# Decay factors of a state-space scan on ScalarE, a mask kept in PSUM, and a logits product widened from 64 to 128 rows

## The chip, the core and the metric

The kernel runs on one core of one Trainium2 chip. TensorE, VectorE, ScalarE, GpSimd and SyncE each work through their own queue in order; in this kernel every DMA is issued from SyncE's queue. The metric is the device time of one launch in microseconds.

## What is computed

One layer of a hybrid encoder is evaluated for 512 prompt tokens and 32 sample tokens that share the weights: an input projection, a banded attention with 16 heads of 64 columns (A), a Mamba-2 state-space scan with 32 heads in 4 groups (B), gates and an output projection, a convolutional feed-forward part and a last gated product. Two pieces matter here. The scan, per chunk and group, is

```python
acs = jnp.cumsum(ac, axis=1)
seg = acs[:, :, None] - acs[:, None, :]
decay = jnp.where(tri, jnp.exp(jnp.where(tri, seg, 0.0)), 0.0)
cb = jnp.einsum('bign,bjgn->bijg', cc, bc)
y = jnp.einsum('bijg,bijgr,bjgrp->bigrp', cb, decay, dx)
y = y + jnp.einsum('bign,bgrpn->bigrp', cc, hc) * jnp.exp(acs)[..., None]
```

and the attention logits are

```python
logits = jnp.einsum('bihd,bjhd->bhij', q, k) * (HEAD_DIM_A ** -0.5)
probs = jax.nn.softmax(logits + bias[None], axis=-1)
```

## The kernel before

All large products run on TensorE with activations as features by tokens (128 x 544). A fp32 weight block of 128 x 1024 (a unit) is split into a rounded high part `wh` (ScalarE, line 250) and a rest `wl` (line 254, on VectorE, or on GpSimd for the odd ones of the first 40 units), and each product is three passes: high by high, high by low, low by high (`mm3`, line 273). One chunk of dense work is six such matmuls of 272 columns; a step of eight chunks fills a PSUM tile `dps` (two buffers), which an epilogue then reads. TensorE's order is written out by hand (`Ordered` pins every matmul behind the one before). The order on the other engines, and which buffer of a pool a tile gets, is the framework's choice: it lists instructions by the time at which it thinks they can start.

The scan runs inside the dense work (lines 1128 to 1142). For each of 20 pairs of group and token block, `ssd_a` (line 611) is emitted, then 7 dense chunks, then `ssd_b` (line 663) of the pair before, then 6 dense chunks. `ssd_a` makes C-by-B in a PSUM tile `cbt`, multiplies it by the triangle into `cbm` in SBUF (line 625), splits the transposed B (lines 627 and 628), and then, for each half of 4 heads: loads the cumulated decay rows `ab` by DMA, broadcast to all partitions (line 647); forms `min(ab - acs, 0)` for 4 heads on VectorE (line 651); one exp on ScalarE (line 652); one product with `cbm` on VectorE (line 653); for all but the first block also exp of `ab` and its product with C on GpSimd (lines 657 and 658). `ssd_b` uses these tiles in its matmuls `yps` and `st`. The half tiles (`dx`, `wj`, `wjh`, `wjl`, `ab`, `m`) share 14 buffers; the PSUM tiles `cbt`, `xst`, `yps`, `st` and all small ones later share 4 buffers (`sps`, line 172).

The attention follows, again between dense chunks (lines 1144 to 1169). For a pair of heads m, `stack` (line 806) builds `qs` (the rounded query in one half of the 128 rows, its rest in the other half) and `ks` (the rounded key in both halves, the second copied there by DMA), and `kl` (the key's rest, in the head's own 64 rows, line 820). One tile `kl` serves both heads. `att_a` (line 823) makes the logits of a block of 128 queries and n = 256, 384 or 512 keys with two matmuls per head: `qs` by `ks` on 128 rows (line 848) and `qs` by `kl` on the head's own 64 rows (line 849), both into the same PSUM tile. The softmax, the transposes (`att_b`) and the product with V (`att_c`) come in later slots, with dense chunks between them (`FILL`).

`bias_vector` (line 551) builds a vector of relative-position biases once, in a constant tile `er`, and writes it to DRAM (`evec`).

Of the kernel before, what the change touches and what calls it, by code (L numbers as in the profile page):

```python
# [9 lines left out]
F32 = mybir.dt.float32  # L10
F32R = mybir.dt.float32r
AF = mybir.ActivationFunctionType
ALU = mybir.AluOpType
MUL, ADD, SUB, MAX, MIN = ALU.mult, ALU.add, ALU.subtract, ALU.max, ALU.min
# [16 lines left out]
EROW = 640  # L31
# [85 lines left out]
def trunk(ctx: ExitStack, tc: tile.TileContext, a):  # L117
    nc = tc.nc
    V, S, G = nc.vector, nc.scalar, nc.gpsimd
# [15 lines left out]
    PE = Ordered()  # L135
# [4 lines left out]
    const = ctx.enter_context(tc.tile_pool(name="const", bufs=1))  # L140
# [6 lines left out]
    pools = {"sp": sp_stack.enter_context(tc.tile_pool(name="sp", bufs=1))}  # L147
# [6 lines left out]
    def slot(dt=F32, name="t", src=None):  # L154
        src = free_slots if src is None else src
        pool, i = src.popleft()
        t = pool.tile([128, T], dt, tag=f"t{i}", name=name, bufs=1)
        held[id(t)] = (t, pool, i, src)
        return t

    def done(*ts):
        for t in ts:
            _, pool, i, src = held.pop(id(t))
            src.append((pool, i))
# [10 lines left out]
    def spt(shape, tag, bufs):  # L175
        return pools["sp"].tile(shape, F32, tag=tag, name=tag, bufs=bufs)
# [372 lines left out]
        dense.defer(4, bias_vector)  # L549

    def bias_vector():
        er = const.tile([16, EROW], F32, name="er")
        nc.sync.dma_start(er[:, 383:EROW], a["rb"])
        V.tensor_scalar(er[:, 383:EROW], er[:, 383:EROW], -1.0, None, op0=MUL)
        V.tensor_copy(er[:, 0:383], er[:, 383:384].to_broadcast([16, 383]))
        nc.sync.dma_start(evec, er)
        for h in range(16):
            dense.defer(16 + 16 * h, lambda h=h: bias_rows(h))

# [51 lines left out]
    def ssd_a(g, c):  # L611
        q0 = 128 * c
        Q = 128 if c < 4 else SMP
        tk = slice(q0, q0 + Q)
        b, cc = bc["B", g], bc["C", g]
        if c == 4:
            hst = spt([128, 512], "h", 4)
            nc.sync.dma_start(hst, a["hT"][:, 512 * g : 512 * g + 512])
            state[g, "s"] = hst
        inter = c != 0  # L620
        sm = sps("cbt")
        PE.matmul(sm[:Q, 0:Q], lhsT=b[:, tk], rhs=cc[:, tk], start=True, stop=True)
        PE.transpose(sm[:Q, 128:256], b[:, tk], ident)
        cbm = spt([128, 128], "cbm", 2)
        V.tensor_tensor(cbm[:Q, :Q], sm[:Q, 0:Q], tri[:Q, :Q], op=MUL)
        bth, btl = (pools["sp"].tile([128, 128], F32R, tag=n, name=n, bufs=2) for n in ("bth", "btl"))
        S.copy(bth[:Q], sm[:Q, 128:256])
        V.tensor_tensor(btl[:Q], sm[:Q, 128:256], bth[:Q].bitcast(F32), op=SUB)
        xp = sps("xst")
        for i in range(4):  # L630
            PE.transpose(xp[:Q, 128 * i : 128 * i + 128], xs[4 * g + i][:, tk], ident)
        dx = half_tile("dx")
        wj = half_tile("wj")
        xv = xp.rearrange("p (h f) -> p h f", f=64)
        for dst, i in ((dx, 0), (wj, 2)):
            V.tensor_tensor(dst.rearrange("p a (b f) -> p (a b) f", f=64)[:Q], xv[:Q],  # L636
                            tm[:Q, i, c, 8 * g : 8 * g + 8].unsqueeze(2).to_broadcast([Q, 8, 64]), op=MUL)
        dxf = dx.rearrange("p a b -> p (a b)")
        wjh, wjl = half_tile("wjh", F32R), half_tile("wjl", F32R)
        S.copy(wjh[:Q], wj[:Q])  # L640
        G.tensor_tensor(wjl[:Q], wj[:Q], wjh[:Q].bitcast(F32), op=SUB)
        sts = [(l[:Q], r.rearrange("p a b -> p (a b)")[:Q]) for l, r in ((bth, wjh), (bth, wjl), (btl, wjh))]
        ms, cps = [], []
        for hh in range(2):
            ab = half_tile("ab")
            src = asc[c, 8 * g + 4 * hh : 8 * g + 4 * hh + 4, 0:Q]
            nc.sync.dma_start(ab[:, :, :Q], src.unsqueeze(0).to_broadcast([128, 4, Q]))
            m = half_tile("m")
            for i in range(4):
                hd = 8 * g + 4 * hh + i  # L650
                V.tensor_scalar(m[:Q, i, :Q], ab[:Q, i, :Q], tm[:Q, 1, c, hd : hd + 1], 0.0, op0=SUB, op1=MIN)  # L651
            S.activation(m[:Q, :, :Q], m[:Q, :, :Q], AF.Exp)  # L652
            V.tensor_tensor(m[:Q, :, :Q], m[:Q, :, :Q],  # L653
                            cbm[:Q, :Q].unsqueeze(1).to_broadcast([Q, 4, Q]), op=MUL)
            ms.append(m)
            if inter:
                S.activation(ab[:, :, :Q], ab[:, :, :Q], AF.Exp)  # L657
                G.tensor_tensor(ab[:, :, :Q], ab[:, :, :Q],  # L658
                                cc[:, tk].unsqueeze(1).to_broadcast([128, 4, Q]), op=MUL)
                cps.append(ab)  # L660
        return dxf, sts, ms, cps
# [122 lines left out]
    bias = {}  # L784

    def att_load(m):
        if m not in att:
            att[m] = slot(name="at", src=at_slots)
        if m % 2 == 0:
            bs = qk["bs", m] = apt([128, NKS], "bs", 1)  # L790
            for p in range(2):
                ck = qk["ck", m + p] = apt([128, PAST], "ck", 2)
                nc.sync.dma_start(ck, a["ck"][m + p])
                cv = qk["cv", m + p] = apt([128, 2, 128], "cv", 2)
                nc.sync.dma_start(cv, a["cv"][m + p])
            for j in range(4):
                nc.sync.dma_start(bs[32 * j : 32 * j + 32], toeplitz(2 * m + j, SMP, 255, NKS))
        for hi in range(2):
            b = apt([128, 512], "bias", 4)
            nc.sync.dma_start(b, toeplitz(2 * m + hi, 128, 127, 512))  # L800
            G.memset(b[0:64, 448:512], -NEG)
            bias[m, hi] = b

    stk = {}

    def stack(m, hi):
        q, k = qk["q", m], qk["k", m]

        def st(n, tag):
            return pools["ap"].tile([128, n], F32R, tag=tag, name=tag, bufs=1)  # L810

        kl = st(512, "kl") if hi == 0 else stk[0][2]
        a0, b0 = 64 * hi, 64 - 64 * hi
        own, oth = slice(a0, a0 + 64), slice(b0, b0 + 64)
        qs, ks = st(384, f"qs{hi}"), st(512, f"ks{hi}")
        S.copy(ks[own], k[own, 0:512])
        nc.sync.dma_start(ks[oth].bitcast(F32), ks[own].bitcast(F32))
        S.copy(qs[own], q[own, 128:512])
        V.tensor_tensor(qs[oth], q[own, 128:512], qs[own].bitcast(F32), op=SUB)
        G.tensor_tensor(kl[own], k[own, 0:512], ks[own].bitcast(F32), op=SUB)  # L820
        stk[hi] = qs, ks, kl

    def att_a(m, i):
        q, k = qk["q", m], qk["k", m]
        if i < 0:
            L = sps("Ls")
            for s in (0, 1):
                for j in range(4):
                    mm, own = m + j // 2, slice(64 * (j % 2), 64 * (j % 2) + 64)
                    r = qk["k", mm][own, SEQ:T] if s else qk["ck", mm][own, :]  # L830
                    PE.matmul(L[32 * j : 32 * j + 32, PAST if s else 0 : NKS if s else PAST],
                              lhsT=qk["q", mm][own, SEQ:T], rhs=r, start=True, stop=True)
            P = apt([128, NKS], "Ps", 1)
            softmax(P, L[:, :NKS], qk["bs", m], 128)
            return [P]
        n = 128 * (i + 1)
        Ps = []
        Ls = []
        for hi in range(2):
            p0 = 64 * hi  # L840
            L = sps("L")
            own = slice(p0, p0 + 64)
            if i == 0:
                PE.matmul(L[:, :n], lhsT=q[own, 0:n], rhs=k[own, 0:n], start=True, stop=True)
            else:
                qs, ks, kl = stk[hi]
                sl = slice(n - 256, n - 128)
                PE.matmul(L[:, :n], lhsT=qs[:, sl], rhs=ks[:, 0:n], start=True, stop=False)
                PE.matmul(L[:, :n], lhsT=qs[own, sl], rhs=kl[own, 0:n], start=False, stop=True)
            Ls.append(L)  # L850
        for hi in range(2):
            P = apt([128, 512], "P", 4)
            softmax(P[:, :n], Ls[hi][:, :n], bias[m, hi][:, 512 - n : 512], 128)
            Ps.append(P)
        return Ps
# [289 lines left out]
            (1, 0): (4, 3), (1, 1): (3, 4), (1, 2): (4, 3), (1, 3): (1, 3)}  # L1145
    todo = [(m, i) for m in range(NPAIR) for i in range(-1 + m % 2, 4)]
    prev = None
    att_load(0)
    stack(0, 0)
    dense.run(11)  # L1150
# [113 lines left out]
```

## Time and profile before

| what | value |
|---|---|
| median of three runs | 1412.58 us (1412.04 to 1417.83) |
| profiled execution, its own time | 1413.28 us |
| its span, first to last instruction | 1411.2 us |
| busy: TensorE, VectorE, ScalarE, GpSimd | 98%, 65%, 43%, 25% of the span |
| mean granted clock of TensorE | 0.991 of 2.4 GHz |

The busy share of TensorE is modelled from pipelined matmuls, so it is read by stages, and beside it the distance from the start of one matmul to the start of the next. Three stages are told apart here: the scan (74 to 381 us), the attention (381 to 640 us) and the dense rest.

### The profile page before, as it was taken

To read this page: it belongs to the slowest core of one execution; us is meant where nothing else is said; L and a number is where in the kernel's file an instruction comes from. 1 tells how busy PE (TensorE), PEld (TensorE's weight loads), DVE (VectorE), ACT (ScalarE), POOL (GpSimd) and SP (SyncE) were. 2 spreads that over 40 slices of the span, in tenths; PEclk is the share of its full clock that TensorE was granted. 3 is DMA by queue.
4 is the path that set the end of the run, shared out by engine and by line. 5 is a ranking of instruction groups with operands and counts; after the bars stand their busy time and mean duration, and the time that the engine had idled before them with its cause. 6 is when DMAs were issued, how large, how long until landed. Compare 5 with 4: busy or idle time off the path is not lost.

```text
span 1411.2 us, 26759 instructions
## 1 busy us (share of the span) xinstructions
PE 1376.0 (98%) x11065; PEld 1324.1 (94%) x11065; DVE 916.0 (65%) x1654; ACT 613.4 (43%) x1016; POOL 352.1 (25%) x464
## 2 busy tenths in 40 slices
PE   7998898989999999999999999999999999999998
PEld 7997897989988888889999999999999999999998
DVE  7999999996865555564355334577777537753545
ACT  5444343455566666654244223344444214432342
POOL 5466475464422112210000000023333103310000
PEclk9999999999999999999999999999999999999999
DMA  5723232323443323311222332222222232222221
GB/s 175 241 90 109 87 120 64 116 92 110 132 138 114 103 88 99 103 64 61 90 91 90 122 122 90 91 78 79 85 88 91 90 106 90 91 93 90 90 90 65
DMA packets 41929, 142.16 MB, mean 101 GB/s; under 512 B 9264, under 2 KB 13248, under 8 KB 29520
## 3 DMA queue, kind: packets, MB, share of 16 engines
q1 hardware_dynamic: 41808, 140.46, 29.6%
q8 instruction: 87, 1.43, 0.4%
q14 instruction: 34, 0.28, 0.1%
HBM read 129.27 MB, written 14.31 MB: 102 GB/s over the span
## 4 chain that ended last, share of the span: by engine, by line
PE 81%; DVE 13%; DMA 2%; ACT 2%; issue 1%; POOL 1%; SPq 0%; POOLq 0%; ACTq 0%
PE dps L130 72%; DVE m L651 3%; PE L L130 3%; DVE cv L597 2%; PE O L130 2%; DMA ab<-asc 2%; PE Tp L133 1%; DVE m L653 1%; DVE wl L254 1%; PE yps L130 1%; DVE xs L684 1%; DVE dx L636 1%; DVE wj L636 0%; PE qn L130 0%; DVE h L693 0%
## 5 line engine op out<-in xcount | busy, mean ns | idle before, releaser
L130 PE MATMUL dps<-hi,wh 128*128 128x272 f32 x2960 | 627.9, 294 | 14.9 <-DVE ext L572 14.6
L130 PE MATMUL dps<-lo,wh 128*128 128x272 f32 x2960 | 616.2, 290 | 5.3 <-DVE lo L375 5.3
L130 PE MATMUL dps<-hi,wl 128*128 128x272 f32 x2960 | 615.4, 290 | 2.3 <-DVE wl L254 1.9
L130 PEld LDWEIGHTS dps<-hi,wh 128*128 128x128 f32 x2960 | 467.4, 190 | 26.2 <-issue 18.5
L130 PEld LDWEIGHTS dps<-lo,wh 128*128 128x128 f32 x2960 | 469.0, 190 | 6.1 <-DVE lo L375 6.1
L130 PEld LDWEIGHTS dps<-hi,wl 128*128 128x128 f32 x2960 | 467.8, 189 | 3.1 <-DVE wl L254 2.5
L250 ACT CAST wh<-wr 128x1024 fp32r<-128x1024 f32 x192 | 201.2, 1048 | 379.3 <-PE dps L130 339.4
L254 DVE TENSOR_TENSOR wl<-wr,wh 128x1024 fp32r<-128x1024 f32 x173 | 213.3, 1233 | 48.2 <-ACT wh L250 43.3
L597 DVE SCALAR_TENSOR_TENSOR cv<-ext,hv,cv 128x547 f32<-128x547 f32 x72 | 76.9, 1068 | 2.7 <-ACT cv L594 2.1
L1021 DVE SCALAR_TENSOR_TENSOR ucv<-uext,vec,ucv 128x546 f32<-128x546 f32 x96 | 75.4, 785 | 4.2 <-ACT ucv L1018 2.4
L1014 POOL COPY cfo<-uext 128x2 f32<-128x2 f32 x48 | 10.4, 217 | 262.4 <-DVE uext L571 262.4
L1011 POOL MEMSET uext<- 128x2 f32 x48 | 4.6, 95 | 281.2 <-issue 281.2
L1053 DVE TENSOR_TENSOR x<-x,dps 128x544 f32<-128x544 f32 x24 | 17.3, 722 | 78.2 <-PE dps L130 78.0
L651 DVE TENSOR_SCALAR m<-ab,tm 128x128 f32<-128x128 f32 (+1 forms) x160 | 63.2, 452 | 5.3 <-DMA ab<-asc 5.3
L777 DVE CUSTOM_DVE_ANT_0 P<-L,bias 128x128 f32<-128x128 f32 (+3 forms) x64 | 30.9, 483 | 53.7 <-PE L L130 53.2
L569 DVE TENSOR_TENSOR uext<-dps,rstd 128x272 f32<-128x272 f32 x48 | 21.2, 442 | 63.1 <-PE dps L130 58.5
L254 POOL TENSOR_TENSOR wl<-wr,wh 128x1024 fp32r<-128x1024 f32 x19 | 50.8, 2672 | 44.8 <-ACT wh L250 36.8
L1015 POOL COPY cfo<-uext 128x2 f32<-128x2 f32 x48 | 55.5, 1157 | 0.0
L658 POOL TENSOR_TENSOR ab<-ab,bc 128x512 f32<-128x512 f32 (+1 forms) x32 | 42.5, 1332 | 40.1 <-ACT ab L657 37.8
L652 ACT ACTIVATE m<-m 128x512 f32<-128x512 f32 (+1 forms) x40 | 22.7, 567 | 65.8 <-DVE m L651 65.6
L733 POOL TENSOR_TENSOR ql<-qs,qh 128x544 fp32r<-128x544 f32 x16 | 22.0, 1376 | 103.6 <-ACT qh L732 91.6
L779 ACT ACTIVATE P<-P,sm 128x128 f32<-128x128 f32 (+3 forms) x64 | 36.0, 562 | 23.2 <-DVE sm L777 22.9
(246 smaller groups left out, 1626.4 us busy)
## 6 DMA issues: line engine op xcount, KB each, us to landing
wr<-in_w SPq DMA_DIRECT2D x96, 1024.0 KB, 4.9
ab<-asc SPq DMA_DIRECT2D x32, 256.0 KB, 5.5
bsc<-evec SPq DMA_DIRECT2D x16, 320.0 KB, 7.5
bias<-bsc SPq DMA_DIRECT2D x16, 256.0 KB, 3.5
xin<-in_xT SPq DMA_DIRECT2D x8, 272.0 KB, 5.4
out_o_v<-v SPq DMA_DIRECT2D x8, 272.0 KB, 2.1
out_o_k<-qk SPq DMA_DIRECT2D x8, 272.0 KB, 2.1
x<-in_xT SPq DMA_DIRECT2D x8, 272.0 KB, 4.6
```

Source lines behind the costliest of these rows:

```text
L130: return self._pin(nc.tensor.matmul(*args, **kw))
L250: cp = S.copy(hi, r)
L254: eng.tensor_tensor(lo, r, hi.bitcast(F32), op=SUB)
L597: V.scalar_tensor_tensor(y[:, :n], ext[:, j : j + n], hv[:, 24 * j + ti : 24 * j + ti + 1], y[:, :n], op0=MUL, op1=ADD)
L651: V.tensor_scalar(m[:Q, i, :Q], ab[:Q, i, :Q], tm[:Q, 1, c, hd : hd + 1], 0.0, op0=SUB, op1=MIN)
L652: S.activation(m[:Q, :, :Q], m[:Q, :, :Q], AF.Exp)
L658: G.tensor_tensor(ab[:, :, :Q], ab[:, :, :Q], cc[:, tk].unsqueeze(1).to_broadcast([128, 4, Q]), op=MUL)
L733: G.tensor_tensor(lo[:, :T], sq[:, :T], hi[:, :T].bitcast(F32), op=SUB)
L777: V.tensor_tensor_reduce(out=P, in0=L, in1=B, scale=1.0, scalar=3e38, op0=ADD, op1=MIN, accum_out=nm[:n])
L779: S.activation(P, P, AF.Exp, scale=-1.0, bias=nm[:n], accum_out=sm[:n])
L1015: G.tensor_copy(cfo[:, i, 2:4], ext[:, UW - 2 : UW])
L1021: V.scalar_tensor_tensor(y[:, :n], ext[:, j : j + n], vec[:, V_FW + 48 * j + i : V_FW + 48 * j + i + 1], y[:, :n], op0=MUL, op1=ADD)
```

## The change

Four edits. In `ssd_a`, the four VectorE operations of a half (subtract, then minimum with zero) become four ScalarE activations Relu(acs - ab), with the per-partition `acs` as bias and scale -1, and the exp that follows gets scale -1, so that the value is the same. `cbm` is no longer an SBUF tile: the triangle is multiplied onto the C-by-B product inside its PSUM tile, and line 653 reads it there. In the attention the tile of key rests becomes two tiles `klz`, one per head of the pair, zeroed once by GpSimd; the head's own half is written as before, and the second logits matmul runs on all 128 rows, where the other half of `kl` holds zeros. `bias_vector` uses two short-lived slots in place of a constant tile, and writes the vector with two DMAs.

```diff
     def bias_vector():
-        er = const.tile([16, EROW], F32, name="er")
-        nc.sync.dma_start(er[:, 383:EROW], a["rb"])
-        V.tensor_scalar(er[:, 383:EROW], er[:, 383:EROW], -1.0, None, op0=MUL)
-        V.tensor_copy(er[:, 0:383], er[:, 383:384].to_broadcast([16, 383]))
-        nc.sync.dma_start(evec, er)
+        er, e0 = slot(name="er"), slot(name="e0")
+        nc.sync.dma_start(er[0:16, 0:257], a["rb"])
+        V.tensor_scalar(er[0:16, 0:257], er[0:16, 0:257], -1.0, None, op0=MUL)
+        V.tensor_copy(e0[0:16, 0:383], er[0:16, 0:1].to_broadcast([16, 383]))
+        nc.sync.dma_start(evec[:, 0:383], e0[0:16, 0:383])
+        nc.sync.dma_start(evec[:, 383:EROW], er[0:16, 0:257])
+        done(er, e0)
...
-        cbm = spt([128, 128], "cbm", 2)
-        V.tensor_tensor(cbm[:Q, :Q], sm[:Q, 0:Q], tri[:Q, :Q], op=MUL)
+        cbm = sm[:, 0:128]
+        V.tensor_tensor(cbm[:Q, :Q], cbm[:Q, :Q], tri[:Q, :Q], op=MUL)
...
-                V.tensor_scalar(m[:Q, i, :Q], ab[:Q, i, :Q], tm[:Q, 1, c, hd : hd + 1], 0.0, op0=SUB, op1=MIN)
-            S.activation(m[:Q, :, :Q], m[:Q, :, :Q], AF.Exp)
+                S.activation(m[:Q, i, :Q], ab[:Q, i, :Q], AF.Relu, scale=-1.0, bias=tm[:Q, 1, c, hd : hd + 1])
+            S.activation(m[:Q, :, :Q], m[:Q, :, :Q], AF.Exp, scale=-1.0)
...
+    klz = []
+
+    def lo_tiles():
+        for hi in range(2):
+            t = pools["ap"].tile([128, 512], F32R, tag=f"klz{hi}", name=f"klz{hi}", bufs=1)
+            G.memset(t.bitcast(F32), 0.0)
+            klz.append(t)
...
-        kl = st(512, "kl") if hi == 0 else stk[0][2]
+        kl = klz[hi]
...
-                PE.matmul(L[:, :n], lhsT=qs[own, sl], rhs=kl[own, 0:n], start=False, stop=True)
+                PE.matmul(L[:, :n], lhsT=qs[:, sl], rhs=kl[:, 0:n], start=False, stop=True)
...
+    lo_tiles()
     att_load(0)
```

## Rows read from the trace of the kernel before

**Rows 1.** Busy time by stage: stretch, length, then busy us (instructions) per engine.

```profile
74.00:381.00 307.00, 283.91 (x2385) 267.51 (x2384) 285.84 (x568) 139.16 (x233) 172.26 (x160) 0.97 0.31 102
381.00:640.00 259.00, 258.63 (x2083) 227.16 (x2082) 148.86 (x369) 161.95 (x388) 51.06 (x50) 1.00 0.32 101
```

**Rows 2.** Waits of TensorE, 50 to 450 us: total us, times, longest.

```profile
PE dps L130 <- DVE ext L572: 14.2, 6, 4.4
PE cbt L130 <- DVE xs L684: 2.3, 1, 2.3
```

**Rows 3.** The view of rows 1 in two slices of 20 us.

```profile
240.00:260.00 20.00, 16.36 (x110) 15.40 (x111) 17.51 (x42) 7.22 (x11) 7.58 (x9) 0.74 0.31 106
...
340.00:360.00 20.00, 19.91 (x177) 18.93 (x178) 14.45 (x37) 10.71 (x21) 10.92 (x7) 1.00 0.42 143
```

**Rows 4.** TensorE in time (start, us, what): first C-by-B matmul of four `ssd_a`.

```profile
74.28 0.25 PE L130 MATMUL cbt<-bc 128*32 128x32 f32 x2
...
192.13 0.38 PE L130 MATMUL cbt<-bc 128*128 128x128 f32 x2
...
205.48 0.38 PE L130 MATMUL cbt<-bc 128*128 128x128 f32 x2
...
360.92 0.38 PE L130 MATMUL cbt<-bc 128*128 128x128 f32 x2
```

**Rows 5.** Groups, 60 to 380 us: count, busy us, mean ns, idle before, what ended it.

```profile
L651 DVE TENSOR_SCALAR m<-ab,tm 128x128 f32<-128x128 f32 (+1 forms) x160 | 63.2, 452 | 5.3 <-DMA ab<-asc 5.3
...
L653 DVE TENSOR_TENSOR m<-m,cbm 128x512 f32<-128x512 f32 (+1 forms) x40 | 33.4, 838 | 2.3 <-ACT m L652 2.2
...
L652 ACT ACTIVATE m<-m 128x512 f32<-128x512 f32 (+1 forms) x40 | 22.7, 567 | 65.8 <-DVE m L651 65.6
```

**Rows 6.** Single durations on three lines: ns minimum/median/maximum, first and last start.

```profile
L651 DVE TENSOR_SCALAR m<-ab,tm x160: 219/275/3675, 82.3 to 373.1; 128x128 f32<-128x128 f32 x128, 32x32 f32<-32x32 f32 x32
...
L653 DVE TENSOR_TENSOR m<-m,cbm x40: 271/682/2203, 84.1 to 375.0; 128x512 f32<-128x512 f32 x32, 32x128 f32<-32x128 f32 x8
...
L693 DVE TENSOR_TENSOR h<-h,st x16: 667/675/683, 98.3 to 381.0; 128x512 f32<-128x512 f32 x16
```

**Rows 7.** Groups of ScalarE, shapes kept apart, columns as in rows 5.

```profile
L779 ACT ACTIVATE P<-P,sm 128x128 f32<-128x128 f32 x16 | 6.4, 402 | 5.5 <-DVE sm L777 5.5
...
L652 ACT ACTIVATE m<-m 32x128 f32<-32x128 f32 x8 | 2.5, 308 | 12.1 <-DVE m L651 12.1
```

**Rows 8.** ScalarE in time: two activations back to back.

```profile
191.09 0.63 ACT L652 ACTIVATE m<-m 128x512 f32<-128x512 f32 x1 [2.64 <-DVE m L651]
191.63 0.61 ACT L657 ACTIVATE ab<-ab 128x512 f32<-128x512 f32 x1
```

**Rows 9.** Waits of SyncE's queue, 60 to 390 us, columns as in rows 2.

```profile
SPq L237 <- POOL wl L254: 94.1, 14, 12.5
```

**Rows 10.** DMA issues: count, KB each, median us from issue to landing.

```profile
ab<-asc SPq DMA_DIRECT2D x32, 256.0 KB, 5.5
```

**Rows 11.** VectorE in time: the second mask product of the `ssd_a` begun at 192.13.

```profile
208.74 1.62 DVE L653 TENSOR_TENSOR m<-m,cbm 128x512 f32<-128x512 f32 x1
```

**Rows 12.** TensorE in time: four logits matmuls of 512 keys, and what follows.

```profile
407.07 0.49 PE L130 MATMUL L<-ks,qs 128*128 128x512 f32 x1
407.49 0.49 PE L130 MATMUL L<-kl,qs 64*128 64x512 f32 x1
...
408.78 0.39 PE L130 MATMUL dps<-hi,wh 128*128 128x272 f32 x1
```

**Rows 13.** TensorE in time: matmuls of one shape in a row.

```profile
187.16 0.39 PE L130 MATMUL st<-wjl,bth 128*128 128x512 f32 x1
187.39 0.39 PE L130 MATMUL st<-wjh,btl 128*128 128x512 f32 x1
...
414.21 0.49 PE L130 MATMUL L<-qk 64*128 64x128 f32 x4
```

**Rows 14.** The second logits matmul: count, ns minimum/median/maximum, first and last start, shapes.

```profile
L130 PE MATMUL L<-kl,qs x48: 380/438/502, 396.6 to 630.5; 64*128 64x256 f32 x16, 64*128 64x384 f32 x16, 64*128 64x512 f32 x16
```

## The prediction

> **What bounds the kernel now.** I read the busy time by stage first, then TensorE's waits, then the starts of single matmuls. In the attention TensorE is busy without a gap, in the scan it is not: 283.9 of 307 us, at a mean granted clock of 0.97, while VectorE is busy for 285.8 us, 93% [rows 1]. So in the scan it is VectorE that TensorE waits for, and the wait that ends last says where: dense products wait for the epilogue's reads of their PSUM tile, 14.2 us in six waits [rows 2]. The slices show both ends: at 240 us TensorE works 16.4 of 20 us and its clock falls to 0.74, a mix of 2.4 and 1.2 GHz after idling; at 340 us, where VectorE is busy for 14.5 us only, TensorE has 19.9 [rows 3].
>
> How much can be had there? Idle time is 307 - 283.9 = 23.1 us, and a clock of 0.97 loses another 3% of 307, 9.2 us: 32.3 us. The starts give the same by another way: from the first to the last `ssd_a` there are 19 intervals in 360.92 - 74.28 = 286.6 us, and an undisturbed one, 192.13 to 205.48, takes 13.35 us [rows 4]. 19 x 13.35 = 253.7, so 32.9 us are lost. I take 33 us as the most that any relief of VectorE can return.
>
> In the attention the loss isn't idle time. Four logits matmuls of 512 columns start 0.42 to 0.44 us apart, 1.71 us from the first to the next dense matmul [rows 12]; three state matmuls of the same 512 columns, also added up in one bank, start 0.23 us apart [rows 13]. The four alternate between 128 and 64 rows; those of the state do not. Four matmuls that all have 64 rows pass in 0.49 us together [rows 13], so 64 rows in themselves cost nothing. The extra 0.2 us comes at each change of the row count.
>
> **The change, part by part.** (1) *Relu on ScalarE.* VectorE loses 160 operations, 63.2 us busy [rows 5]. That is more than their work: the median is 275 ns and the mean 452, with a maximum of 3675 [rows 6]; the long ones are held up, while a VectorE operation that reads PSUM, the state's sum, never leaves 667 to 683 ns [rows 6]. ScalarE gains 160 activations. The nearest row with a per-partition bias and 128 columns takes 402 ns [rows 7], without the bias 308 ns [rows 7]; back to back, starts lie about 0.09 us closer than the duration (0.54 against 0.63) [rows 8]. I take 0.31 us for 128 columns and 0.23 for the 32 of the sample block (the difference by 0.84 ns per column, from 0.63 us at 512 [rows 8] and 0.308 at 128 [rows 7]): 128 x 0.31 + 32 x 0.23 = 47 us. The bounds are 0.22 and 0.40 each, 35 to 64 us. ScalarE goes from 139 [rows 1] to 186 us. It has the room: it stands idle for 65.6 us in front of the exp, waiting for just these VectorE results [rows 5]. A wait moves with the step: the first Relu of a half must wait for the `ab` transfer, 5.5 us from issue to landing [rows 10], and behind it in ScalarE's queue stand the weight casts, the conv and tanh steps and the PSUM copies. The transfer is issued behind weight loads on SyncE's queue, which wait 94.1 us for GpSimd's weight split [rows 9]. VectorE met this wait for 5.3 us in all [rows 5], covered by its own backlog; on ScalarE more of it will show. It starts later than the wait it replaces ended only where the transfer is later than VectorE's own queue was, so I count nothing for it in the sum and keep it as a rival.
>
> The Trainium skill ("ScalarE: Activation LUTs", section "Rules for kernel authors") advises VectorE, not ScalarE, for relu and min. The rows agree that the single step gets no shorter; by that rule the edit is a loss, and only the question of who waits for whom speaks for it.
>
> (2) *Mask in PSUM.* Line 653 reads two SBUF tensors, takes 682 ns at the median, 2203 at most and 33.4 us in all [rows 5, 6]. With one operand in PSUM it has the form of the state's sum, 675 ns with hardly a spread. 32 x 0.68 + 8 x 0.27 = 23.9 us, so 9.5 us less. The multiplication that writes PSUM has no like in the trace; between 0.1 us less and 0.28 more for each of 20, -2 to +6 us, I take +1. What it costs is a buffer: one of four PSUM buffers is held until the second half's product (below).
>
> VectorE then has 285.8 - 63.2 - 9.5 + 1 = 214 us of work in a stage of about 282, 76%. That is the share of the slice at 340 us (14.5 of 20, 72%), where TensorE lost 0.1 us in 20 [rows 3]. The conv epilogues lie in the first two thirds, where I expect nearer 85%. I leave a quarter of the loss standing, 8 us: a gain of **25 us**, with bounds of 8 and 33.
>
> (3) *128 rows.* 48 second logits matmuls [rows 14], two heads at a time, make 24 groups of four; each now has four changes of row count (into 64, back, into 64, back to the dense work). 24 x 4 x 0.2 = **19 us**, all on TensorE in a stage where it is never idle [rows 1]. The streamed columns stay the same, and the zero rows cost none. VectorE and ScalarE are busy 149 and 162 of 259 us there [rows 1], so they can follow at 240. The bounds are 0 and 20. The two zeroings of 128 x 512 come once, on a GpSimd that is busy for 51 of 259 us [rows 1].
>
> The Trainium skill ("TensorEngine Tiling (Array Packing)", section "Key Properties") says that changing the tiling mode, not just the tile, drains the engine. The trace agrees: about 0.2 us at each change.
>
> (4) *Bias vector.* Two more short transfers and two slots, once, long before they are read: nothing, at most the second DMA's issue on SyncE's queue.
>
> **Sum.** The profiled execution took 1413.28 us, of which 1411.2 is its span; 1413.3 - 25 - 19.2 = 1369.1. It lies 0.7 us above the median of the runs, so I say **1368 us**.
>
> **The rivals.** *ScalarE takes VectorE's place.* Its in-order queue stands before a Relu whose `ab` has not landed; a late cast then delays weights, and TensorE waits for `wh` or `wl` in place of the epilogue. For it: the loads behind GpSimd's weight split [rows 9]. Against it: two thirds busy at most, and 65.6 us of such standing are in the trace already [rows 5]. It would leave 8 us of the 33: 1413 - 8 - 19 = 1386 us.
>
> *The logits don't speed up.* Either the 0.2 us has another cause, or the softmax chain becomes what the shorter groups wait for. Against it stand rows 12 and 13 side by side. 1413 - 25 - 0 = 1388 us.
>
> *PSUM holds TensorE up.* This one ends slower. `cbt`, `xst`, `yps` and `st` are four tiles per iteration and there are four buffers; `cbt` used to be free after the B split, and now stays until line 653 of the second half. If the next C-by-B matmul needs that very buffer, TensorE waits for it with all dense work behind it. In the iteration begun at 192.13 [rows 4] the second product ends at 210.36 [rows 11], 18.2 us later, where the mean interval is 286.6 / 19 = 15.1. Were that lag to stay, 19 x 3.1 = 59 us come on top: 1413 + 59 - 19 = 1453 us. It decides as soon as the lag exceeds the 13.35 us of an undisturbed interval. For it: a C-by-B matmul waited for a buffer once already, 2.3 us [rows 2]. Against it: the lag is VectorE's backlog, which goes; and another buffer may be free, `xst` above all, which is read early.
>
> *Relu isn't in the loaded table*, and each half pays two table loads: ScalarE would be full and eat the scan's gain, about 1405 to 1415 us. The skill page on ScalarE (section "Table sets: the hidden batching unit") lists relu as filler in every set; no run here shows it yet.
>
> **How the numbers follow.** My forecast has a chance of 0.62; ScalarE in VectorE's place 0.17; no gain in the logits 0.10; PSUM 0.05; the table or several partial failures together 0.06. The range takes the bounds of the two gains: both near full (33 + 20) give 1360, and I allow for a few us beyond; the first two rivals give 1386 and 1388. So 1356 to 1390. About 0.5%, 7 us, is what a measurement of this kernel can tell from no change. The first three cases are faster by more: 0.89; the table case is about the same: 0.06; PSUM is slower: 0.05.
>
> **What would show it.** Right: logits matmuls of 512 columns 0.23 us apart; `ssd_a` intervals near 13.4 us; VectorE near 76% in the scan with no wait of dense products for `ext`; line 653 without long ones; Relu starts 0.31 us apart. Wrong: TensorE's waits now ending on ScalarE's `wh` or `th`, a `cbt` or `xst` matmul waiting for line 653 or 684, or logits starts that stay 0.42 us apart.

## The result, and the profile after

The changed kernel takes 1368.87 us (median of four runs, 1368.12 to 1370.15) against 1412.94 us of the kernel before in the same series: a ratio of 0.968, with a 95% interval of 0.966 to 0.971. The forecast was 1368. The profiled execution has a span of 1367.7 us, 43.5 us less than before.

The busy time by stage comes first (columns as in rows 1): the scan, now 74 to 354 us, and the attention, now 354 to 596 us. The third line is the scan measured from its first to its last C-by-B matmul, the same stretch that the prediction divided into 19 intervals.

```profile
74.00:354.00 280.00, 276.04 (x2377) 263.65 (x2375) 225.48 (x406) 181.58 (x393) 165.31 (x159) 0.98 0.34 112
354.00:596.00 242.00, 240.46 (x2077) 224.76 (x2076) 151.96 (x367) 160.35 (x388) 49.85 (x51) 1.00 0.34 108
...
73.47:335.71 262.24, 258.28 (x2209) 246.72 (x2209) 213.59 (x384) 169.23 (x368) 155.35 (x152) 0.97 0.34 114
```

From first to last C-by-B matmul the scan took 286.6 us [rows 4] and takes 262.2: 24.4 us less. From the first to the last logits matmul with the key's rest the attention took 630.5 - 396.6 = 233.9 us [rows 14]; the line of that matmul (columns as in rows 14) now gives 587.5 - 369.5 = 218.0, 15.9 less:

```profile
L130 PE MATMUL L<-klz,qs x48: 278/336/397, 369.5 to 587.5; 128*128 128x256 f32 x16, 128*128 128x384 f32 x16, 128*128 128x512 f32 x16
```

These two make 40.3 of the 43.5 us. The rest lies before the scan (0.8), between the two stretches (1.9) and behind them (0.5).

TensorE's waits from 50 to 450 us (columns as in rows 2) no longer name the epilogue's `ext`; six waits of 14.2 us are gone [rows 2]. What is left, beside two waits of 0.4 and 0.2 us:

```profile
PE st L130 <- ACT qs L746: 2.6, 1, 2.6
PE qn L130 <- DVE xs L686: 1.1, 1, 1.1
```

The two slices that answer to rows 3 lie at 240 us again and, for the quiet end of the scan, at 320 us. TensorE's 16.4 us at a clock of 0.74 have become 20 at full clock, though VectorE is still busy for 16.9 (17.5 before):

```profile
240.00:260.00 20.00, 20.00 (x179) 19.09 (x179) 16.92 (x27) 13.34 (x29) 13.21 (x9) 1.00 0.40 134
...
320.00:340.00 20.00, 20.00 (x177) 19.54 (x176) 11.27 (x21) 13.07 (x27) 10.38 (x8) 1.00 0.41 135
```

The groups that answer to rows 5, 60 to 360 us. Line 653 is now the Relu, 654 the exp, 655 the mask product; 714 is a VectorE step of the scan's gate that the change does not touch.

```profile
L653 ACT ACTIVATE m<-ab,tm 128x128 f32<-128x128 f32 (+1 forms) x160 | 48.3, 372 | 11.6 <-DMA ab<-asc 11.5
...
L655 DVE TENSOR_TENSOR m<-m,cbt 128x512 f32<-128x512 f32 (+1 forms) x40 | 24.0, 599 | 19.7 <-ACT m L654 19.7
L654 ACT ACTIVATE m<-m 128x512 f32<-128x512 f32 (+1 forms) x40 | 22.4, 560 | 0.5
...
L714 DVE SCALAR_TENSOR_TENSOR z<-zt,z 128x544 f32<-128x544 f32 x8 | 11.7, 1456 | 3.0 <-ACT zt L713 3.0
```

The wait has changed sides. Before, ScalarE stood idle for 65.6 us in front of the exp, waiting for VectorE [rows 5]; now VectorE stands 19.7 us in front of the product, waiting for the exp, and the exp waits for next to nothing (0.5 us). Single durations (columns as in rows 6) show what PSUM does to the product: its longest took 2203 ns [rows 6], and now no product leaves the median by more than 14 ns upwards.

```profile
L653 ACT ACTIVATE m<-ab,tm x160: 304/387/403, 79.6 to 344.8; 128x128 f32<-128x128 f32 x128, 32x32 f32<-32x32 f32 x32
...
L655 DVE TENSOR_TENSOR m<-m,cbt x40: 267/676/690, 82.7 to 346.7; 128x512 f32<-128x512 f32 x32, 32x128 f32<-32x128 f32 x8
```

ScalarE in time (as in rows 8): four Relu take 1.26 us together, so their starts lie (1.26 - 0.387) / 3 = 0.29 us apart.

```profile
190.24 1.26 ACT L653 ACTIVATE m<-ab,tm 128x128 f32<-128x128 f32 x4
191.53 0.63 ACT L654 ACTIVATE m<-m 128x512 f32<-128x512 f32 x1
```

The logits group of 512 keys (as in rows 12) passes in 407.09 - 406.07 = 1.02 us, against 1.71 [rows 12]:

```profile
406.07 0.50 PE L130 MATMUL L<-ks,qs 128*128 128x512 f32 x1
406.40 0.40 PE L130 MATMUL L<-klz,qs 128*128 128x512 f32 x1
406.63 0.39 PE L130 MATMUL L<-ks,qs 128*128 128x512 f32 x1
406.86 0.39 PE L130 MATMUL L<-klz,qs 128*128 128x512 f32 x1
407.09 0.41 PE L130 MATMUL dps<-hi,wh 128*128 128x272 f32 x2
```

Three of its four distances are 0.23 us; the first one is 0.33. The dense matmuls behind the group gain as well: their first two start 0.35 us before the next two in the kernel before (first two lines), and 0.25 now (the line of 407.09 above, and the third line).

```profile
408.78 0.52 PE L130 MATMUL dps<-hi,wh 128*128 128x272 f32 x2
409.13 0.42 PE L130 MATMUL dps<-lo,wh 128*128 128x272 f32 x2
407.34 0.42 PE L130 MATMUL dps<-lo,wh 128*128 128x272 f32 x2
```

### The profile page after: what moved, and what is told of

The parts are those of the page before. It is cut to its first block, busy times and chain, and to the rows that moved or that the text cites. A ratio compares the mean times of both kernels' runs of the same rounds, so it can differ in the third digit from the quotient of the medians.

```text
span 1367.7 us, 26737 instructions
## 1 busy us (share of the span) xinstructions
PE 1350.5 (99%) x11065; PEld 1317.8 (96%) x11065; DVE 858.5 (63%) x1494; ACT 654.3 (48%) x1176; POOL 345.1 (25%) x466
## 4 chain that ended last, share of the span: by engine, by line
PE 91%; DVE 4%; ACT 2%; DMA 1%; issue 1%; POOL 0%; SPq 0%; DVEq 0%; ACTq 0%; POOLq 0%
PE dps L130 80%; PE O L130 2%; PE yps L130 2%; PE L L130 2%; PE Tp L133 1%; PE st L130 1%; DMA ab<-asc 1%; DVE cv L599 1%; DVE qs L828 1%; ACT wh L250 0%; ACT m L653 0%; PE xst L133 0%; PE gps L130 0%; PE qn L130 0%; DMA wr<-in_w 0%
## 5 line engine op out<-in xcount | busy, mean ns | idle before, releaser
L599 DVE SCALAR_TENSOR_TENSOR cv<-ext,hv,cv 128x547 f32<-128x547 f32 x72 | 73.1, 1015 | 7.2 <-ACT cv L596 6.6
L1023 POOL COPY cfo<-uext 128x2 f32<-128x2 f32 x48 | 11.5, 240 | 261.7 <-DVE uext L573 261.7
L653 ACT ACTIVATE m<-ab,tm 128x128 f32<-128x128 f32 (+1 forms) x160 | 48.3, 372 | 11.6 <-DMA ab<-asc 11.5
L368 ACT CAST hi<-me 128x544 fp32r<-128x544 f32 x24 | 15.5, 647 | 62.0 <-DVE me L1048 62.0
L1027 ACT ACTIVATE ucv<-uext,vec 128x546 f32<-128x546 f32 x48 | 40.7, 847 | 7.0 <-DVE uext L574 2.5
```

The costliest lines, as they stand in the source:

```text
L599: V.scalar_tensor_tensor(y[:, :n], ext[:, j : j + n], hv[:, 24 * j + ti : 24 * j + ti + 1], y[:, :n], op0=MUL, op1=ADD)
L653: S.activation(m[:Q, i, :Q], ab[:Q, i, :Q], AF.Relu, scale=-1.0, bias=tm[:Q, 1, c, hd : hd + 1])
L1027: S.activation(y[:, :n], ext[:, 0:n], AF.Identity, scale=vec[:, V_FW + i : V_FW + i + 1], bias=vec[:, V_FB + i : V_FB + i + 1])
```

## The experiments

The theory is the prediction's: in the scan TensorE waited for VectorE, so VectorE's relief is worth its share of the lost time; in the attention each change of the row count costs TensorE time of its own. The kernel before took 1412.9 to 1415.8 us in the different series, so each ratio is against the kernel before in its own series, with its 95% interval.

### The three edits one at a time

First, the logits edit on the kernel before.

```diff
-        kl = st(512, "kl") if hi == 0 else stk[0][2]
+        kl = klz[hi]
...
-                PE.matmul(L[:, :n], lhsT=qs[own, sl], rhs=kl[own, 0:n], start=False, stop=True)
+                PE.matmul(L[:, :n], lhsT=qs[:, sl], rhs=kl[:, 0:n], start=False, stop=True)
```

> The kernel before with the logits edit alone (two zeroed tiles for the key rests, second logits matmul on 128 rows). Theory: TensorE pays about 0.2 us at each change between 128-row and 64-row matmuls and is never idle in the attention, so 24 groups of four lose 0.67 to 0.8 us each: 16 to 19 us, 1394 to 1397 us; the scan's intervals stay at 15.1 us. Rival: the distance of 0.42 us has another cause, or the softmax chain takes the gain back: 1409 to 1413 us.

It took 1396.93 us, ratio 0.986 (0.985 to 0.988). The scan from first to last C-by-B matmul stayed at 286.5 us, and so did the waits in it:

```profile
PE dps L130 <- DVE ext L572: 14.5, 6, 4.5
```

From the first to the last product with the key's rest the attention took 218.1 us, 15.8 less, the same as in the full change (15.9):

```profile
L130 PE MATMUL L<-klz,qs x48: 279/336/397, 396.9 to 615.0; 128*128 128x256 f32 x16, 128*128 128x384 f32 x16, 128*128 128x512 f32 x16
```

So the scan's part and the attention's part of the change do not touch each other. The medians give more than the traces: 1415.48 - 1396.93 = 18.6 us, and the three edits alone add up to 50.9 us by their medians, against 44.1 for the whole change. Part of it is the kernel before, which took 1413.24 to 1419.64 us in this series, where the execution of it that was traced took 1413.28. I go by the stretches, since every trace with the same logits products in the same order repeats that of the attention to 0.1 us.

Second, the Relu on ScalarE alone, with the mask in SBUF as before.

```diff
-                V.tensor_scalar(m[:Q, i, :Q], ab[:Q, i, :Q], tm[:Q, 1, c, hd : hd + 1], 0.0, op0=SUB, op1=MIN)
-            S.activation(m[:Q, :, :Q], m[:Q, :, :Q], AF.Exp)
+                S.activation(m[:Q, i, :Q], ab[:Q, i, :Q], AF.Relu, scale=-1.0, bias=tm[:Q, 1, c, hd : hd + 1])
+            S.activation(m[:Q, :, :Q], m[:Q, :, :Q], AF.Exp, scale=-1.0)
```

> The kernel before with Relu on ScalarE alone, the mask still in SBUF. Theory: the 63 us taken from VectorE are the larger part of the scan's gain, 18 to 24 of 25 us: 1389 to 1395 us, and the mask products still show long ones of 1.5 us and more. Rival: ScalarE's wait for the decay rows holds up its casts and returns most of it: 1400 us or more. The attention stays as it was.

It took 1392.47 us, ratio 0.984 (0.982 to 0.985). The scan took 266.9 us, 19.7 less; the attention kept its 233.9 us. The four largest waits of TensorE:

```profile
PE yps L130 <- POOL ab L658: 2.2, 2, 1.1
PE yps L130 <- DVE m L653: 1.9, 1, 1.9
PE dps L130 <- POOL wl L254: 1.8, 2, 1.7
PE dps L130 <- DVE ext L572: 1.7, 1, 1.7
```

The 14.2 us for `ext` have become 1.7, and three others of about 2 us stand ahead of them. None of the four names ScalarE. So this edit alone brings most of the scan's gain.

Third, the mask product in PSUM alone, with the subtraction still on VectorE.

```diff
-        cbm = spt([128, 128], "cbm", 2)
-        V.tensor_tensor(cbm[:Q, :Q], sm[:Q, 0:Q], tri[:Q, :Q], op=MUL)
+        cbm = sm[:, 0:128]
+        V.tensor_tensor(cbm[:Q, :Q], cbm[:Q, :Q], tri[:Q, :Q], op=MUL)
```

> The kernel before with the mask in PSUM alone; VectorE keeps its decay factors and so its backlog, with the second mask product about 18 us behind the C-by-B matmul. Theory: the products with the mask lose their stretch, 9.5 us less on VectorE, and the next C-by-B matmul gets another of the four buffers: 1403 to 1411 us. Rival: TensorE now waits at the next C-by-B or transposes for the held buffer, 3 us in each of 19 intervals: 1425 to 1470 us.

It took 1406.15 us, ratio 0.993 (0.991 to 0.994); the scan took 279.5 us, 7.1 less. The line of the mask product, the scan's line (columns as in rows 1) and the two largest waits:

```profile
L653 DVE TENSOR_TENSOR m<-m,cbt x40: 266/676/689, 82.5 to 366.1; 128x512 f32<-128x512 f32 x32, 32x128 f32<-32x128 f32 x8
72.95:352.42 279.47, 262.00 (x2209) 248.97 (x2208) 255.77 (x534) 128.91 (x215) 153.76 (x150) 0.96 0.33 107
```

```profile
PE xst L133 <- DVE xs L684: 8.7, 2, 5.2
PE dps L130 <- DVE ext L572: 6.9, 3, 4.0
```

The product loses its long ones, and the waits for `ext` halve. Against these 7.3 us stands a new wait of 8.7: the transposes `xst` wait until line 684 has read `yps`. All in all TensorE is idle for 17.5 us of the scan (279.47 - 262.00), where the kernel before had 21.9 in the same stretch. With one of the four PSUM buffers held by `cbt`, the transposes get the buffer that the `ssd_b` before them still uses. This is the prediction's PSUM rival in a small form. It did not hang on line 653, as the rival's sum put it, but on the next user of the pool; the wait for line 684 is one of the prediction's signs of being wrong.

### The mask's buffer on top of the Relu

Then the changed kernel with the mask back in an SBUF tile, the third edit undone.

> The changed kernel with the mask back in an SBUF tile. Theory: VectorE's mask products are held up again, 5 to 9 us more on an engine that is 80% busy in the scan; the scan gets 3 to 6 us longer: 1371 to 1376 us. Rival: the PSUM buffer that the mask holds still costs TensorE something, and without it the kernel is faster: 1362 to 1367 us.

It took 1374.81 us, ratio 0.970 (0.968 to 0.972). The scan took 266.4 us, 4.2 more than in the first profile of the changed kernel, and the long products came back:

```profile
L655 DVE TENSOR_TENSOR m<-m,cbm x40: 271/694/2375, 84.0 to 353.3; 128x512 f32<-128x512 f32 x32, 32x128 f32<-32x128 f32 x8
```

The intervals of the ratios overlap (the changed kernel has 0.968, 0.966 to 0.971), so the total time alone can't tell this gain from none. The scan stretches can a little better: 262.2, 264.0 and 262.4 us in three profiles with the mask in PSUM (two of the changed kernel, one of the padded kernel below), 266.4 and 266.9 in two with it in SBUF. I read 2 to 5 us.

### Giving VectorE its load back

If VectorE's load is the cause, and not something else that came with the Relu, then 160 VectorE operations of the same size put back must bring the old waits back. The first try reads a constant tile into a scratch tile that nobody uses.

```diff
                 S.activation(m[:Q, i, :Q], ab[:Q, i, :Q], AF.Relu, scale=-1.0, bias=tm[:Q, 1, c, hd : hd + 1])
+                scr = spt([128, 128], "scr", 2)
+                V.tensor_scalar(scr[:Q, :Q], ident[:Q, :Q], tm[:Q, 1, c, hd : hd + 1], 0.0, op0=SUB, op1=MIN)
```

> The changed kernel with VectorE's 160 old operations put back as idle work: the same operation and shape, read from a constant tile, written to a scratch tile that nobody reads. Theory: the scan's gain comes from VectorE having less to do; loaded again it is full, and most of the 24 us go: 1385 to 1395 us, with dense products waiting for ext again. Rival: the gain comes from the shorter chain, all of it on ScalarE, and VectorE's load matters little: 1369 to 1375 us.

It took 1405.57 us, ratio 0.992 (0.990 to 0.994), beyond the range that was expected. The scan took 295.8 us, 9 more than in the kernel before. The waits for `ext` are back, but the added operations did not lie where the old ones lay:

```profile
PE dps L130 <- DVE ext L574: 16.9, 6, 6.0
PE xst L133 <- DVE xs L688: 6.5, 2, 4.1
PE xst L133 <- DVE m L657: 1.3, 1, 1.3
```

```profile
L655 DVE TENSOR_SCALAR scr<-ident,tm x160: 218/270/2489, 65.3 to 227.7; 128x128 f32<-128x128 f32 x128, 32x32 f32<-32x32 f32 x32
```

Since they depend on nothing that comes late, the framework listed them early: all 160 ran by 227.7 us, where the subtractions of the kernel before were spread up to 373.1 [rows 6]. The first half of the scan was overloaded. In the third wait line 657 is the mask product: here TensorE did wait for the mask's own buffer, 1.3 us, as the PSUM rival had it. The run supports the theory in kind but not in size, so I ran it again with the operation reading `ab`, as the old one did:

```diff
+                scr = spt([128, 128], "scr", 2)
+                V.tensor_scalar(scr[:Q, :Q], ab[:Q, i, :Q], tm[:Q, 1, c, hd : hd + 1], 0.0, op0=SUB, op1=MIN)
```

> The changed kernel with VectorE's 160 old operations put back as idle work, this time reading the decay rows as the old ones did, so that they stand where they stood (in a2_dveload all of them had run before 228 us, crowded into the first half of the scan). Theory: VectorE's load sets the scan; with the old load at the old place, and the mask in PSUM, it comes back to what e3_psum had, intervals of 275 to 283 us in all, 1383 to 1392 us. Rival: the chain through ScalarE alone is what counts, and the scan stays below 268 us, under 1375 us.

It took 1394.08 us, ratio 0.985 (0.982 to 0.988). The scan took 286.5 us, that of the kernel before to a tenth, with VectorE busy for 262.1 of them (first line; columns as in rows 1). The waits lie elsewhere in part:

```profile
75.29:361.75 286.46, 263.80 (x2208) 249.93 (x2208) 262.05 (x536) 171.60 (x368) 156.60 (x151) 0.96 0.31 104
```

```profile
PE dps L130 <- DVE ext L574: 6.3, 4, 2.6
PE xst L133 <- DVE xs L688: 5.3, 2, 3.1
PE yps L130 <- POOL ab L662: 5.1, 2, 4.3
PE yps L130 <- DVE m L657: 3.6, 2, 2.3
```

All the scan's gain goes when VectorE's 160 operations return, with the Relu still on ScalarE and the mask still in PSUM. The logits' gain stays: 0.985 is what the logits edit gave alone (0.986). It is a little more than expected (1394.08 us, where the range ended at 1392), and the list shows waits that the theory had left out: a late VectorE now also holds up `yps`, through its operands, and `xst`, through line 688. One thing is not load: ScalarE's exp of `ab` has to wait until the added operations have read `ab`, 14.8 us in the trace, and the 5.1 us for GpSimd's product hang on that. In the first try no other engine had to wait for the added operations themselves, and the scan lost more, not less; so VectorE's load suffices to take the gain away.

### How much room ScalarE has

Each Relu done twice, the second time for nothing:

```diff
-                S.activation(m[:Q, i, :Q], ab[:Q, i, :Q], AF.Relu, scale=-1.0, bias=tm[:Q, 1, c, hd : hd + 1])
+                for _ in range(2):
+                    S.activation(m[:Q, i, :Q], ab[:Q, i, :Q], AF.Relu, scale=-1.0, bias=tm[:Q, 1, c, hd : hd + 1])
```

> The changed kernel with every Relu done twice over the same output: 160 more activations, about 47 us, and ScalarE 82% busy in the scan. Theory: ScalarE has the room, and only the chain of a half gets 1.2 us longer: 1369 to 1374 us. Rival: ScalarE's queue has become the next bound, with casts behind the Relus: 1380 us or more, and TensorE waiting for wh or wl.

It took 1376.58 us, ratio 0.971 (0.970 to 0.973), some 5 us more than the changed kernel (0.0032 of 1413, 4.5 us, by the ratios, whose intervals overlap; 6.3 us by the scan's 268.6, and 4.6 against the 264.0 of the changed kernel's second profile). The scan's line and the largest wait:

```profile
75.16:343.74 268.58, 260.37 (x2209) 248.00 (x2209) 213.20 (x384) 207.50 (x520) 156.98 (x151) 0.97 0.34 111
```

```profile
PE yps L130 <- POOL ab L661: 6.5, 2, 3.7
```

Of some 40 us of added work on ScalarE (207.5 - 169.2 = 38.3) four to six reach the end. TensorE waits for GpSimd's product of `ab` with C, which needs ScalarE's exp of `ab`, queued behind the Relus; it still waits for no `wh` or `wl`. At 77% ScalarE begins to be late here; at the 65% of the changed kernel (169.2 of 262.2) this wait is missing. The median lies a little above the range that the theory named; by the ratio, 0.9714 of the first series' 1412.94 us is 1372.5, inside it.

### What the change of row count costs

If the cost sits at the change of the row count, the old 64-row products should lose part of it when the four are only put in another order: both 128-row products first, then both 64-row ones. This is the kernel before with nothing else changed.

```diff
                 PE.matmul(L[:, :n], lhsT=qs[:, sl], rhs=ks[:, 0:n], start=True, stop=False)
-                PE.matmul(L[:, :n], lhsT=qs[own, sl], rhs=kl[own, 0:n], start=False, stop=True)
             Ls.append(L)
+        for hi in range(2 if i else 0):
+            qs, ks, kl = stk[hi]
+            own = slice(64 * hi, 64 * hi + 64)
+            sl = slice(n - 256, n - 128)
+            PE.matmul(Ls[hi][:, :n], lhsT=qs[own, sl], rhs=kl[own, 0:n], start=False, stop=True)
```

> The kernel before with the order of the four logits matmuls changed and nothing else: both 128-row ones first, then both 64-row ones. Theory: two changes of the row count per group in place of four, 24 x 2 x 0.17 to 0.2 us: 8 to 10 us less, 1403 to 1405 us; the second matmul of each kind starts 0.23 us behind the first at 512 keys. Rival: a 64-row product costs its 0.2 us wherever it stands, or the cost is that of adding to a bank just written: 1411 to 1414 us.

It took 1404.02 us, ratio 0.992 (0.990 to 0.993); the logits stretch went from 233.9 to 223.0 us, 10.9 less (first line). TensorE in time, a group of 512 keys, from 410.9 us:

```profile
L130 PE MATMUL L<-kl,qs x48: 379/437/498, 401.7 to 624.7; 64*128 64x256 f32 x16, 64*128 64x384 f32 x16, 64*128 64x512 f32 x16
```

```profile
411.02 0.73 PE L130 MATMUL L<-ks,qs 128*128 128x512 f32 x2
411.68 0.50 PE L130 MATMUL L<-kl,qs 64*128 64x512 f32 x2
412.11 0.52 PE L130 MATMUL dps<-hi,wh 128*128 128x272 f32 x2
```

With two changes fewer per group, the four pass in 412.11 - 411.02 = 1.09 us, almost the 1.02 of the widened product. Order alone, with the same instructions, takes away most of the loss, so it does not belong to 64 rows in themselves. Nor does it belong to adding to a bank just written, the other rival: in the changed kernel the fourth product adds to the bank of the third and starts 0.23 us behind it (406.63 and 406.86). The second line of this group shows more than was expected: the two 64-row products, one on rows 0 to 63 and one on rows 64 to 127, stand in it with one start and pass in 412.11 - 411.68 = 0.43 us together, what one of them took before [rows 12]. So of the 0.62 us saved (1.71 - 1.09) two changes at 0.2 us make some 0.4, and the two products side by side the other 0.2.

The Trainium skill ("TensorEngine Tiling (Array Packing)", section "Key Properties") says that different tiles operate independently and that a change of mode drains the engine. Both agree with these lines: two 64-row products in 0.43 us, and 0.2 us at a change.

### Clock falls after the sample block

In the profile of the changed kernel TensorE's clock falls to 0.50 (1.2 GHz) for three to four microseconds at 93, 161 and 229 us, without TensorE having been idle. Each comes some three microseconds after the small matmuls of a sample block begin (32 tokens, at 90, 158 and 226 us); a fourth at 314 us lies behind the idle wait of 2.6 us shown above. To see whether the small matmuls are the cause, I padded them to 128 rows and 128 columns with zeros.

```diff
-                          lhsT=dxf[:Q, 64 * hd : 64 * hd + 64], rhs=ms[hd // 4][:Q, hd % 4, :Q],
+                          lhsT=dxf[:, 64 * hd : 64 * hd + 64], rhs=ms[hd // 4][:, hd % 4, :],
```

> The changed kernel with the sample block's output matmuls made as large as the others: 128 rows and 128 columns, the rest zeros, with four zeroings by GpSimd per group and no more instructions on TensorE. In the changed kernel TensorE's clock falls to 0.50 for 4 us some 2 us behind each of three such blocks, without TensorE having been idle. Theory: the small matmuls, 32 rows by 32 columns, are what precedes the fall, and with full ones these three falls are gone, about 2 us each: 1362 to 1366 us and a mean clock of 0.996 or more. Rival: the falls have another cause and stay: 1368 to 1371 us, or more by the zeroings that GpSimd adds.

It took 1368.42 us, ratio 0.966 (0.964 to 0.967), and its profile has none of the three falls. That looked like a small gain, so the changed kernel itself was run again, unaltered.

> The changed kernel as it is, beside the run above and the kernel before on the same chip, to set a4_fill and a1_sbufmask against it: a ratio of 0.966 to 0.971 to the kernel before. If the full sample block of a4_fill (0.9655) was a gain, this ratio lies at 0.968 or above; if not, the two agree within 0.002.

It took 1370.51 us, ratio 0.967 (0.965 to 0.970). The two intervals overlap almost entirely, and in this second profile of the very same program the three falls are missing too. The first two lines are of the first profile, the next two of the second, columns as in rows 1:

```profile
93.00:94.00 1.00, 1.00 (x5) 1.00 (x6) 1.00 (x2) 0.97 (x2) 1.00 (x1) 0.50 0.45 172
94.00:95.00 1.00, 1.00 (x6) 1.00 (x6) 1.00 (x4) 1.00 (x4) 0.86 (x4) 0.50 0.03 8
```

```profile
93.00:94.00 1.00, 1.00 (x9) 0.64 (x7) 1.00 (x4) 0.64 (x1) 0.37 (x1) 1.00 0.94 336
94.00:95.00 1.00, 1.00 (x8) 0.91 (x8) 1.00 (x2) 0.82 (x3) 0.95 (x1) 1.00 0.63 240
```

So nothing is shown of the small matmuls as a cause; what makes the falls come in one execution and not in another stays open. Nor do the times of this run's six executions follow the mean granted clock: the four at 0.993 took 1366.66 to 1371.39 us, the two at 0.996 and 0.997 took 1371.73 and 1372.38. The second profile pays in another coin, six short waits of `xst` for line 686, the PSUM wait again:

```profile
PE xst L133 <- DVE xs L686: 4.4, 6, 1.0
```

Without the first profile's three falls its scan took 264.0 us, not less.

## Why the prediction was right, and where its steps were off

**The bound.** It held as far as it was tested: taking 160 operations off VectorE brought 19.7 us alone, and putting 160 back took the whole gain of 24.4 us away. That the rest of the 33 us was VectorE's doing too is not shown. As a ceiling the 33 us rest in part on luck: one interval of 13.35 us stood for all 19, which in the changed kernel run from 10.5 to 17.2 us. Idle time and clock gave the same 32 us without it.

**The scan's 25 us.** Measured 24.4 (22.6 in the second profile). The Relu alone gave 19.7 and the mask alone 7.1, 26.8 by themselves; together they give a little less, as one expects where both take from the same 33 us.

**VectorE's work** was mis-sized, although the gain came out. The prediction subtracted 63.2 + 9.5 - 1 = 71.7 us from 285.8 and got 214 us, 76%. Measured are 225.5 us in the scan's stage, 60.4 less, and 81%. The two numbers were of different kinds. A group's busy time counts in full what overlaps with the instructions of other groups: the busy times of all 24 groups of VectorE in the stage of before add up to 317.0 us, while the engine's own is 285.8 [rows 1]. The 63.2 and 9.5 us were taken from such groups. The sum over the groups did fall as counted, by 70.0 us (to 247.0, 23 groups); the engine's busy time fell by 9.6 us less, because the doubly counted time fell too, from 31.2 to 21.5 us. The mask product was right, 24.0 against 23.9 us. Held-up time also moved between the lines that were left: the gate's line 714 went from 7.0 us (as line 712) to 11.7, the weight split of line 254 from 23.5 to 25.2, while the convolution's line 599 fell from 58.4 (as line 597) to 54.6.

**The 8 us left standing.** 262.2 - 253.7 = 8.5 us. The size fits; of what it would be made the prediction did not say. There are no waits for `ext` in it, as its signs had it. What remains are 4.0 us of idle time (262.24 - 258.28), 2.6 of them one wait that the next paragraph explains, and a clock of 0.97, or in the second profile the waits of `xst`.

**ScalarE.** 48.3 us for the Relus against 47, starts 0.29 us apart against 0.31. The step that could have gone wrong, the wait for `ab`, grew from 5.3 us [rows 5] to 11.5, as feared, with transfers that land as fast as before (5.5 us [rows 10] and 5.2). The prediction put the cost of this wait at nothing in its sum, and that was 2.6 us too little: TensorE's longest wait in the scan, for line 746, comes from it.

```profile
312.73 1.28 ACT L653 ACTIVATE m<-ab,tm 128x128 f32<-128x128 f32 x4 [1.71 <-DMA ab<-asc]
313.92 0.84 ACT L746 ACTIVATE qs<-qn,eps 128x272 f32<-128x272 f32 x2
314.44 0.50 PE L130 MATMUL st<-wjh,bth 128*128 128x512 f32 x1 [2.58 <-ACT qs L746]
```

ScalarE's queue stood 1.71 us in front of a Relu whose `ab` had not landed. Behind the four Relus stood line 746, whose operands, the PSUM tile `qn`, had been ready since 310.1 us; and TensorE's `st` needed the buffer that line 746 reads. It is the rival's mechanism, through a PSUM buffer in place of `wh`. The wait stands in the second profile and in the padded kernel too (2.9 and 2.2 us), and in none of the three traced kernels that have only one of the scan's two edits. That ScalarE takes VectorE's place altogether is out at 65% busy; doubling the Relu shows its beginning, 4 to 6 us at 77%.

**The logits' 19.2 us** were right as a price, and some of it came back. That the loss lies at the changes is borne out by the reordered kernel, whose 64-row products stayed. Up to the next dense matmul a group saves 0.69, 0.68 and 0.67 us (medians at 512, 384 and 256 keys), since the first distance, 0.42 us before [rows 12] and 0.33 now, gives only 0.1: the matmuls ahead of the group are those of `O`, on 64 columns of the array, and I take it that the group's first product still pays for that change. The missing 0.1 us per group lies behind it, where the first dense matmuls came 0.35 us apart and now come 0.25. That makes 24 x (0.68 + 0.11) = 19 us. But the stretch got only 15.9 us shorter. Put beside each other matmul by matmul, the two traces show the other side: 2.6 us more in front of and within the products of `O`. In three places `O` now waits for line 884, ScalarE's copy of the prompt's transposed probabilities, as it never did before (waits from 350 to 600 us; the products behind each wait start slowly too):

```profile
PE O L130 <- ACT PT L884: 1.3, 3, 0.4
```

So the step that was off is "so they can follow at 240": the rival that the softmax chain becomes what the shorter groups wait for came in part, and had no term in the sum.

**Why the total fits.** The logits term was 3.3 us too large for want of that wait, the scan term 0.6; against them stand the 0.8, 1.9 and 0.5 us of the rest, 3.2 in sum, which were not forecast. So the 1368 us are partly luck of some 3 us.

**PSUM.** The rival that would have ended slower did not come, but its mechanism is real: 8.7 us of waits in the kernel with the mask alone, 4.4 in the second profile of the changed kernel. Both are waits of `xst` for line 684 (now 686), which the prediction had named as a sign of being wrong; they were too short to make it so. Of its two reasons against the rival, that another buffer may be free is the one that counts. The lag came down with VectorE's backlog, from 14 to 27 us behind the first C-by-B matmul to 12 to 18, but it still exceeds the 13.35 us of an interval in most places, and TensorE waits for line 655 nowhere. In the kernel with the mask alone the lag reached 24 us, and no C-by-B matmul waited.

**The table.** No additional table load appears: 12 before and 12 now. The Trainium skill ("ScalarE: Activation LUTs", section "Table sets: the hidden batching unit") lists relu as filler in every set, and the trace agrees. The Trainium skill's advice of VectorE for relu ("ScalarE: Activation LUTs", section "Rules for kernel authors") would have kept this part of the kernel at its old speed: here the measurement decides against it, 0.984 for that edit alone, because TensorE waited for VectorE and hardly for ScalarE (0.2 us between 50 and 450 us).

## What to carry to other kernels

Move work off the engine that the critical one waits for, even to an engine on which it takes longer (387 ns against 275 here), and look at what stands behind it in that engine's queue: here it cost 2.6 us at 65% busy, and some 5 us more at 77%. The busy times of groups of instructions overlap, so their sum overstates what an engine loses with them, here by 9.6 of 70 us. And put matmuls of one row count side by side, or pad them to it with zeros: the padded product started 0.23 us behind the one before it, like any other of 512 columns, and the change between 64 and 128 rows cost about 0.2 us each time. What a shorter group then waits for belongs in the sum.

## What the runs showed of the hardware

Two 64-row matmuls on different halves of the rows, issued one behind the other, pass side by side: 0.43 us for two of 512 columns.

A VectorE product of two SBUF tensors was often held up: with the mask back in SBUF, those of 128 x 512 took up to 1776 ns at a median of 694 over all forty, and those of 32 x 128 up to 2375 ns, where the shortest took 271. The same products with one operand in PSUM never took more than 690 ns. The trace of that kernel shows when: 20 of the 40 products were long, each of them had begun while a GpSimd instruction was running, and each ended a fixed time behind the end of that instruction, 0.54 to 0.55 us at 128 x 512 and 0.14 us at 32 x 128. In the changed kernel 31 of the 40 ran beside GpSimd, and none was long. The Trainium skill ("SBUF — State Buffer", section "SBUF: two separate sides") gives as the reason a port pair that VectorE, reading two SBUF inputs, and GpSimd, reading SBUF, lock against each other for a whole instruction. The rows agree; no run here took GpSimd's work away.

TensorE's clock fell to 1.2 GHz for three to four microseconds at a time while it was busy without a gap, in one execution of the program and not in the next; single falls are no ground for a change of the program.
